# Thirty-two modulation blocks of a two-layer diffusion backbone: TensorE products in the attention stages in place of VectorE sums in the first layer's FFN

## The chip, the cores and the metric

One core of one Trainium2 chip runs the kernel. The metric is device time in microseconds (us) of one execution. Engines are TensorE (PE, its weight loads PEld), VectorE (DVE), ScalarE (ACT), GpSimd (POOL) and SyncE (SP), which here only issues DMAs. DMAs that POOL and ACT issue have queues of their own.

## What is computed

Two layers over 128 context tokens and 512 latent tokens (640 columns, width 1024). Each layer has a modulation vector for each of the two token groups, and all its norms, gates and residual adds use it:

```
mod = silu(cond) @ w_ada + b_ada                # 6 x 1024 values per layer and group
sh1, sc1, g1, sh2, sc2, g2 = split(mod, 6)
h = rmsnorm(x) * (1 + sc1) + sh1
x = x + g1 * (sum_b sigmoid(gate_b) * branch_b(h)) @ w_out     # retention, differential attention, MLA
h = rmsnorm(x) * (1 + sc2) + sh2
x = x + g2 * (silu(h @ w_a) * (h @ w_b)) @ w_ffn_out           # SwiGLU, 22 tiles of 128
```

In the kernel the 6144 values of a layer are 48 blocks of 128 columns of `w_ada`: blocks 0 to 15 are sh1 and sc1, 16 to 23 g1, 24 to 39 sh2 and sc2, 40 to 47 g2.

## The kernel before

Everything is held transposed, features on the 128 partitions, and the 640 tokens in two halves of 320. A large matmul is three products of fp32r parts (hi·hi, hi·lo, lo·hi; `mm3`, L134). A weight piece (512 KB for 1024 columns) is loaded by `load_w` through SP into a ring of three buffers, `raw`; ACT casts it to `whi` (L118) and DVE subtracts to `wlo` (L121), which frees the ring buffer. `whi` and `wlo` are rings of four.

Stages of a layer: MLA attention (with the projections of differential attention, `diff_proj`, as fillers), first branch, differential attention (fillers: gates and retention values), retention, the last branch, `out_proj`, and the FFN. Fillers are generators; `plan` spreads their steps over the points of a stage at which `fill` is called. What a filler yields goes to PSUM bank `G`, of which there is one. A scheduler then decides each engine's order; engines run their own instructions strictly in that order.

Modulation blocks are made in two ways.

- `ada_chunk` (L214 to L226), at the start of the program: four blocks at a time. Eight fp32 products (L218) with the two condition vectors as 32 weight columns (`cs`), two for each of four column groups of TensorE, give 512 columns in `G`. ACT copies that to `ada_r` (L221), four products with a selecting matrix (L224) bring it to columns, DVE adds the bias. First layer, blocks 0 to 15.
- `ada_rows` (L238 to L259): one block at a time on DVE. POOL loads the block transposed (`rawr`, 512 KB); two multiplications by a broadcast condition vector with a running sum (L251, `junk` is the unused product) give the block for both groups.

`ada_rows` is called in each layer's last branch and `out_proj` for blocks 16 to 39 (and 40 to 43 of the first layer), with 1024 columns at a time. Blocks 44 to 47 of the first layer and 0 to 15 and 40 to 47 of the second are made in the first layer's FFN, in halves of 512 columns (two loads of 256 KB, four DVE instructions a block). The second layer's FFN has none.

The FFN (`ffn`, L1228) makes the 22 tiles in parts: after a part's up products (`up`), its down products (`unit`) run between the next part's. Each part adds to the residual `x` on DVE (`x_add`, L1082), from `G` or `O`; a new accumulation there waits for that add. From tile `FFN_CLASSIC` on, `ffn_seven` uses seven products of half size in place of eight. The two layers differ: `FFN_PARTS`, `FFN_HELD` and `FFN_CLASSIC` are tables by layer (seven parts and classic until tile 5 in the first layer, six parts and until tile 4 in the second), so that the loads and sums have room in SBUF.

Of the kernel before, what the change touches and what calls it, by code (L numbers as in the profile page):

```python
# [12 lines left out]
F32 = mybir.dt.float32  # L13
# [8 lines left out]
P = 128  # L22
D = 1024
KT = 8
DEPTH = 2
# [13 lines left out]
FFN_PARTS = (((0, 3), (3, 6), (6, 9), (9, 12), (12, 15), (15, 18), (18, 22)), ((0, 4), (4, 8), (8, 12), (12, 15), (15, 18), (18, 22)))  # L39
FFN_HELD = (6, 7)  # L40
FFN_CLASSIC = (5, 4)
# [10 lines left out]
class Kern:  # L52
# [185 lines left out]
    def ada_rows(self, l, b0, b1, pool, raws, cols, bufs):  # L238

        d = self.dve  # L240
        if l not in self.mod:
            self.mod[l] = self.const.tile([P, 48, 2], F32, name=f"mod{l}")
        mod = self.mod[l]
        part = self.const.tile([P, 48, 2], F32, tag="modp", name="modp", bufs=1) if cols < 1024 else None
        for n in range(b0, b1):
            for c in range(0, 1024, cols):
                raw = raws.tile([P, cols], F32, tag="rawr", name="rawr", bufs=bufs)
                self.pool.dma_start(out=raw, in_=self.io["w_adat"][l, n][:, c:c + cols])
                junk = pool.tile([P, cols], mybir.dt.bfloat16, tag="junk", name="junk")
                for i in range(2):  # L250
                    self.tc.keep_in_program_order(d.scalar_tensor_tensor(  # L251
                        junk, raw, 1.0, self.csr[:, i, c:c + cols], op0=ALU.mult, op1=ALU.mult,
                        accum_out=(part if c else mod)[:, n, i:i + 1]))
            if n == b1 - 1:
                b = self.pv[:, V_ADA + 48 * l + b0:V_ADA + 48 * l + b1]
                if part is not None:
                    d.tensor_tensor(mod[:, b0:b1], mod[:, b0:b1], part[:, b0:b1], op=ALU.add)
                d.tensor_tensor(mod[:, b0:b1], mod[:, b0:b1], b.unsqueeze(2).to_broadcast([P, b1 - b0, 2]), op=ALU.add)
            yield 1  # L259
# [963 lines left out]
    def ffn(self, l, act, x, pool, hook, a, b, mid, us=None):  # L1223
# [21 lines left out]
        def hold(f):  # L1245
            g[f] = (pool.tile([P, T], F32R, tag="ghi", name="ghi", bufs=FFN_HELD[l]), pool.tile([P, T], F32R, tag="glo", name="glo", bufs=FFN_HELD[l]))

# [18 lines left out]
        def up(f):  # L1266
            if us is not None and f >= FFN_CLASSIC[l]:
                W = self.ffn_weights(pool, io["w_ffn_in"][l, f])
                self.fill()
                if f == FFN_CLASSIC[l]:  # L1270
                    self.pin = True
                    self.sctx.close()
                    if l == 1:
                        self.adctx.close()
# [15 lines left out]
        for p, (f0, f1) in enumerate(FFN_PARTS[l]):  # L1290
            nf, lastp = f1 - f0, p == len(FFN_PARTS[l]) - 1

# [18 lines left out]
            for f in range(max(f0, 2), f1):  # L1311
                up(f)
                for _ in range(min(2 if lastp and nf < FFN_HELD[l] - 2 else 3, len(waiting))):
                    waiting.pop(0)()
# [30 lines left out]
    def run(self):  # L1345
# [3 lines left out]
        for l in range(DEPTH):  # L1349
# [12 lines left out]
            with ExitStack() as c2:  # L1362
                pool = self.sb("mla", 1, c2)
                self.plan(37, (self.diff_proj(l, act, pool), 30, 0.0, 1.0))
                self.mla(l, act, yraw, pool, first)
                self.flush()
# [8 lines left out]
            self.plan(23, (self.gates(l, 2, act, m, mp), 16, 0.0, 0.7), (self.ret_values(l, act, mp), 20, 0.6, 0.95))  # L1375
# [22 lines left out]
            def mdone(h):  # L1398
                mact[h] = self.m_split(m, h)
            self.ada_vectors(adp, rp)  # L1400
            self.plan(22, (chain(self.ada_rows(l, 16, 24, adp, rp, 1024, 3), self.ada_rows(l, 24, 40, adp, rp, 1024, 3)), 24, 0.0, 0.9),
                      *([(self.ada_rows(0, 40, 44, adp, rp, 1024, 3), 4, 0.9, 1.0)] if l == 0 else []))
# [6 lines left out]
            us = [fp.tile([P, T], F32, tag=("ghi", "glo")[k % 2], name="us", bufs=FFN_HELD[l]) if k < 6 else  # L1409
# [11 lines left out]
            if l == 0:  # L1421
                self.plan(72, (self.ada_rows(0, 44, 48, adp, fp, 512, 2), 4, 0.0, 0.0277),
                          (chain(self.ada_rows(1, 0, 16, adp, fp, 512, 2), self.ada_rows(1, 40, 48, adp, fp, 512, 2)), 24, 0.12, 0.9))
# [73 lines left out]
def layout(inputs):  # L1497
# [22 lines left out]
    out["w_ada"] = c(np.stack([pieces(wa[:, 512 * j:512 * j + 512], 2) for j in range(4)]).reshape(1, 4, 4, 128, 2, 512))  # L1520
    out["w_adat"] = c(g["w_ada"].transpose(0, 2, 1).reshape(DEPTH, 48, 128, 1024))
# [53 lines left out]
```

## Time and profile before

| | |
|---|---|
| median of 3 runs | 2491.19 us (2485.24 to 2496.12) |
| the profiled execution | 2487.97 us, of which the span from first to last instruction is 2485.8 us |
| busy share: PE, PEld, DVE, ACT, POOL | 96%, 93%, 74%, 44%, 7% |
| mean granted TensorE clock | 0.992 |
| DMA | 250 MB, mean 101 GB/s |

The profile's PE time is that of pipelined matmuls with modelled ends, so 96% does not say that PE never waits; the start of one matmul to the start of the next is what is read below. The first layer runs from 0 to some 1266 us of the span, the second from there to the end.

### The profile page before, as it was taken

To read this page: it belongs to the slowest core of one execution; us is meant where nothing else is said; L and a number is where in the kernel's file an instruction comes from. 1 tells how busy PE (TensorE), PEld (TensorE's weight loads), DVE (VectorE), ACT (ScalarE), POOL (GpSimd) and SP (SyncE) were. 2 spreads that over 40 slices of the span, in tenths; PEclk is the share of its full clock that TensorE was granted. 3 is DMA by queue.
4 is the path that set the end of the run, shared out by engine and by line. 5 is a ranking of instruction groups with operands and counts; after the bars stand their busy time and mean duration, and the time that the engine had idled before them with its cause. 6 is when DMAs were issued, how large, how long until landed. Compare 5 with 4: busy or idle time off the path is not lost.

```text
span 2485.8 us, 43255 instructions
## 1 busy us (share of the span) xinstructions
PE 2383.3 (96%) x16816; PEld 2315.5 (93%) x16816; DVE 1840.8 (74%) x4146; ACT 1092.2 (44%) x2259; POOL 170.9 (7%) x295
## 2 busy tenths in 40 slices
PE   8999999999999999899999999999999999999997
PEld 5999998999998999899999999989999999999997
DVE  5877686566798788888778776865667976777775
ACT  5655565532234333333365664654222353333344
POOL 0000210000110000000000002100001100000001
PEclk9999999999999999999999999999999999999998
DMA  6211321321653333233232122223225512222222
GB/s 263 74 61 62 102 82 56 109 88 60 208 187 114 96 113 115 96 111 116 82 129 71 65 71 97 81 68 107 74 85 195 186 53 86 76 81 79 77 75 72
DMA packets 83180, 250.03 MB, mean 101 GB/s; under 512 B 11200, under 2 KB 24736, under 8 KB 81952
## 3 DMA queue, kind: packets, MB, share of 16 engines
q1 hardware_dynamic: 55008, 164.13, 20.6%
q0 software_dynamic: 21920, 77.17, 9.4%
q10 hardware_dynamic: 6048, 5.98, 0.7%
q8 instruction: 132, 2.16, 0.4%
q14 instruction: 72, 0.59, 0.1%
HBM read 227.01 MB, written 20.22 MB: 99 GB/s over the span
## 4 chain that ended last, share of the span: by engine, by line
PE 73%; issue 11%; DVE 9%; DMA 4%; ACT 3%; POOL 0%; DVEq 0%; POOLq 0%; ACTq 0%
PE G L134 32%; PE S L134 22%; PE Tp L134 4%; DMA rawr<-w_adat 2%; PE O L872 2%; PE S L1122 1%; PE Tp L675 1%; PE S L1121 1%; PE S L1120 1%; DVE wlo L121 1%; DVE junk L251 1%; DVE x L1082 1%; PE O L650 1%; DMA raw<-w_ffn_in 1%; PE O L649 1%
## 5 line engine op out<-in xcount | busy, mean ns | idle before, releaser
L118 ACT CAST whi<-raw 128x1024 fp32r<-128x1024 f32 (+3 forms) x354 | 298.1, 844 | 475.2 <-PE S L134 185.0
L121 DVE TENSOR_TENSOR wlo<-raw,whi 128x1024 fp32r<-128x1024 f32 (+3 forms) x354 | 342.2, 968 | 101.0 <-ACT whi L118 97.3
L134 PE MATMUL G<-whi,hhi 128*128 128x256 f32 x1040 | 299.0, 288 | 4.7 <-DVE rvs L825 2.9
L134 PE MATMUL G<-whi,hlo 128*128 128x256 f32 x1040 | 295.2, 284 | 0.0
L134 PE MATMUL G<-wlo,hhi 128*128 128x256 f32 x1040 | 294.5, 283 | 0.0
L134 PE MATMUL G<-ghi,whi 128*128 128x320 f32 x704 | 223.3, 317 | 26.5 <-DVE x L1082 23.5
L134 PE MATMUL G<-glo,whi 128*128 128x320 f32 x704 | 219.5, 312 | 0.3 <-DVE glo L121 0.3
L134 PE MATMUL G<-ghi,wlo 128*128 128x320 f32 x704 | 219.2, 311 | 0.0
L251 DVE SCALAR_TENSOR_TENSOR junk<-rawr,csr 128x512 bf16<-128x512 f32 (+1 forms) x216 | 204.1, 945 | 16.0 <-DMA rawr<-w_adat 14.3
L134 PE MATMUL S<-hhi,whi 128*128 128x320 f32 x652 | 204.4, 314 | 5.8 <-DVE gt L1049 5.7
L134 PEld LDWEIGHTS G<-whi,hhi 128*128 128x128 f32 x1040 | 198.1, 191 | 8.1 <-DVE rvs L825 3.8
L134 PE MATMUL S<-hhi,wlo 128*128 128x320 f32 x652 | 202.3, 310 | 0.0
L134 PE MATMUL S<-hlo,whi 128*128 128x320 f32 x652 | 202.3, 310 | 0.0
L134 PEld LDWEIGHTS G<-wlo,hhi 128*128 128x128 f32 x1040 | 198.5, 191 | 0.1
L134 PEld LDWEIGHTS G<-whi,hlo 128*128 128x128 f32 x1040 | 198.3, 191 | 0.0
L1082 DVE SCALAR_TENSOR_TENSOR x<-G,mod,x 128x128 f32<-128x128 f32 (+2 forms) x360 | 147.3, 436 | 38.2 <-PE G L134 37.2
L134 PEld LDWEIGHTS G<-ghi,whi 128*128 128x128 f32 x704 | 133.8, 190 | 37.3 <-issue 26.6
L134 PE MATMUL G<-hhi,whi 128*128 128x320 f32 x512 | 161.9, 317 | 5.9 <-DVE x L1082 2.6
L134 PE MATMUL G<-hlo,whi 128*128 128x320 f32 x512 | 158.9, 310 | 0.0
L134 PE MATMUL G<-hhi,wlo 128*128 128x320 f32 x512 | 158.7, 310 | 0.0
L465 DVE TENSOR_REDUCE mx<-S 128x1 f32<-128x640 f32 (+1 forms) x160 | 113.4, 715 | 50.5 <-PE S L843 29.3
L134 PEld LDWEIGHTS G<-glo,whi 128*128 128x128 f32 x704 | 134.0, 190 | 0.7 <-DVE glo L121 0.6
(439 smaller groups left out, 6632.9 us busy)
## 6 DMA issues: line engine op xcount, KB each, us to landing
raw<-w_ffn_in SPq DMA_DIRECT2D x88, 512.0 KB, 3.6
rawr<-w_adat POOLq DMA_DIRECT2D x52, 512.0 KB, 4.2
raw<-w_gate SPq DMA_DIRECT2D x48, 512.0 KB, 3.7
rawr<-w_adat POOLq DMA_DIRECT2D x56, 256.0 KB, 3.3
raw<-w_diff SPq DMA_DIRECT2D x24, 512.0 KB, 3.8
raw<-w_branch SPq DMA_DIRECT2D x24, 512.0 KB, 3.5
raw<-w_ret SPq DMA_DIRECT2D x24, 512.0 KB, 4.0
raw<-w_ffn_out SPq DMA_DIRECT2D x64, 192.0 KB, 2.4
```

The lines of the kernel that those rows point to most:

```text
L118: (eng or self.act).copy(hi, src)
L121: (eng or self.dve).tensor_tensor(lo, src, hi.bitcast(F32), op=ALU.subtract)
L134: ins = self.pe.matmul(*args, **kw)
L251: self.tc.keep_in_program_order(d.scalar_tensor_tensor(junk, raw, 1.0, self.csr[:, i, c:c + cols], op0=ALU.mult, op1=ALU.mult, accum_out=( ...
L465: self.dve.tensor_reduce(mx, sv, axis=AX.XY if len(sv.shape) == 3 else AX.X, op=ALU.max)
L649: self.pe.matmul(o[:, :n], vv, hi, start=i == 0, stop=False)
L650: self.pe.matmul(o[:, :n], vv, lo, start=False, stop=i == m - 1)
L675: self.pe.transpose(t[:, 256 * kb + 128 * i:256 * kb + 128 * i + 128], ps[i][:, 128 * (k0 + kb):128 * (k0 + kb) + 128], self.ident)
L872: pe.matmul(o[:, :128], at[:, 128 * kb:128 * kb + 128], V[:, kb0 + kb, :], start=kb == 0, stop=kb == nk - 1)
L1082: self.dve.scalar_tensor_tensor(x[h][:, n, c0:c1], ps[:, c0:c1], g[:, n, gi:gi + 1], x[h][:, n, c0:c1], op0=ALU.mult, op1=ALU.add)
L1120: self.pe.matmul(o, lh, rh, start=k == 0, stop=False)
L1121: self.pe.matmul(o, lh, rl, start=False, stop=False)
```

## The change

It takes 32 blocks off `ada_rows` and makes them with a new generator, `ada_products`, in groups of four blocks. A group is `ada_chunk`'s arithmetic, but it loads its four pieces (512 KB each, `rawp`) through the same three-buffer ring `raw` that the other weights use, and is a filler in two steps: eight products and the copy, then the selection and the bias. Six groups run in the first layer (four in MLA, two in differential attention), two in the second layer's MLA. The FFN tables become one set, the second layer's, for both. `ada_rows` keeps blocks 16 to 39 of each layer, spread over 21 points of the last branch and `out_proj` in place of 22 times 0.9.

```diff
-FFN_PARTS = (((0, 3), (3, 6), (6, 9), (9, 12), (12, 15), (15, 18), (18, 22)), ((0, 4), (4, 8), (8, 12), (12, 15), (15, 18), (18, 22)))
-FFN_HELD = (6, 7)
-FFN_CLASSIC = (5, 4)
+FFN_PARTS = ((0, 4), (4, 8), (8, 12), (12, 15), (15, 18), (18, 22))
+FFN_HELD = 7
+FFN_CLASSIC = 4
...
+    def ada_products(self, pool, chunks):
+
+        for l, j in chunks:
+            ps = self.G()
+            for i in range(4):
+                raw = self.w.tile([P, 2, 512], F32, tag="raw", name="rawp", bufs=3)
+                self.nc.sync.dma_start(out=raw, in_=self.io["w_adap"][l, j, i])
+                for kk in range(2):
+                    k = 2 * i + kk
+                    g = k % 4
+                    self.pe.matmul(ps[32 * g:32 * g + 32, :], self.cs[:, k, :], raw[:, kk, :],
+                                   start=k < 4, stop=k >= 4, tile_position=(0, 32 * g))
+            r = pool.tile([P, 512], F32, tag="ada_r", name="ada_r", bufs=1)
+            self.act.copy(r, ps)
+            yield 1
+            ps = self.Tp()
+            for c in range(4):
+                self.pe.matmul(ps[:, 2 * c:2 * c + 2], r[:, 128 * c:128 * c + 128],
+                               self.ct[:, C_SEL:C_SEL + 2], start=True, stop=True)
...
-                self.plan(37, (self.diff_proj(l, act, pool), 30, 0.0, 1.0))
+                chunks = ((0, 10), (0, 11), (1, 0), (1, 1)) if l == 0 else ((1, 10), (1, 11))
+                self.plan(37, (self.diff_proj(l, act, pool), 30, 0.0, 1.0), (self.ada_products(pool, chunks), 2 * len(chunks), 0.0, 1.0))
...
+            chunks = ((1, 2), (1, 3)) if l == 0 else ()
...
+                      (self.ada_products(mp, chunks), 2 * len(chunks), 0.0, 0.7))
...
-            self.plan(22, (chain(self.ada_rows(l, 16, 24, adp, rp, 1024, 3), self.ada_rows(l, 24, 40, adp, rp, 1024, 3)), 24, 0.0, 0.9),
-                      *([(self.ada_rows(0, 40, 44, adp, rp, 1024, 3), 4, 0.9, 1.0)] if l == 0 else []))
+            self.plan(21, (chain(self.ada_rows(l, 16, 24, adp, rp), self.ada_rows(l, 24, 40, adp, rp)), 24))
...
-                self.plan(72, (self.ada_rows(0, 44, 48, adp, fp, 512, 2), 4, 0.0, 0.0277),
-                          (chain(self.ada_rows(1, 0, 16, adp, fp, 512, 2), self.ada_rows(1, 40, 48, adp, fp, 512, 2)), 24, 0.12, 0.9))
+                self.plan(0)
```

How the instructions stand on three engines follows. First SP's queue in the first layer's MLA, from the first projection weights on; the names are ring buffers, and a wait on PE or DVE is for the engine that frees the buffer. Before:

```order
L126 DMA raw_840<-w_diff 128x1024 [waits DMAHW5_49,DMAHW2_49,DVE_49]
L126 DMA raw_987<-w_qp 128x768 [waits DMAHW6_49,DMAHW3_49,DVE_49]
L126 DMA raw_1124<-w_qk 128x640 [waits DMAHW7_49,DMAHW4_49,DVE_49]
L126 DMA raw_1195<-w_v 128x512 [waits DMAHW5_49,DMAHW0_49,DVE_49]
L126 DMA raw_1336<-w_diff 128x1024 [waits DMAHW6_49,DVE_49]
```

With the change:

```order
L126 DMA raw_840<-w_diff 128x1024 [waits DMAHW5_49,DMAHW2_49,DVE_49]
L265 DMA rawp_903<-w_adap 128x1024 [waits DMAHW6_49,DMAHW3_49,DVE_49]
L265 DMA rawp_907<-w_adap 128x1024 [waits DMAHW7_49,DMAHW4_49,DVE_49]
L265 DMA rawp_911<-w_adap 128x1024 [waits DMAHW5_49,DMAHW0_49,DVE_49]
L265 DMA rawp_915<-w_adap 128x1024 [waits DMAHW6_49,PE_49]
L126 DMA raw_1006<-w_qp 128x768 [waits DMAHW7_49,PE_49]
L126 DMA raw_1143<-w_qk 128x640 [waits DMAHW0_49,PE_49]
L126 DMA raw_1214<-w_v 128x512 [waits DMAHW1_49,PE_49]
```

A group's first three pieces fill the ring; its fourth, and the three weight loads behind it, wait until PE has used them. The same holds for all eight groups.

Second, PE at the same place of the program with the change: the first group, between transposes of MLA's query (`cqn`), and the first users of `w_qp` (`whi_1008`) and `w_qk` (`whi_1145`).

```order
L269 MATMUL G_902<-rawp_907,cs_86 32x512 [waits DMAHW7_49]
L269 MATMUL G_902<-rawp_907,cs_86 32x512
L269 MATMUL G_902<-rawp_911,cs_86 32x512 [waits DMAHW0_49]
L269 MATMUL G_902<-rawp_911,cs_86 32x512
L576 MATMUL Tp_956<-ct_76,cqn_953 128x128 [waits DVE_49]
L576 MATMUL Tp_956<-ct_76,cqn_953 128x128 x2
L576 MATMUL Tp_969<-ct_76,cqn_966 128x128 [waits DVE_49]
L576 MATMUL Tp_969<-ct_76,cqn_966 128x128 x2
L269 MATMUL G_902<-rawp_915,cs_86 32x512 [waits DMAHW1_49]
L269 MATMUL G_902<-rawp_915,cs_86 32x512
```

Six products stand together, then six transposes, then the two of the fourth piece. In the second layer's first group nothing stands between (`whi_14937` is `w_qk`):

```order
L269 MATMUL G_14916<-rawp_14925,cs_86 32x512 [waits DMAHW2_49]
L269 MATMUL G_14916<-rawp_14925,cs_86 32x512
L269 MATMUL G_14916<-rawp_14929,cs_86 32x512 [waits DMAHW3_49]
L269 MATMUL G_14916<-rawp_14929,cs_86 32x512
L134 MATMUL S_14941<-ckh_14350,whi_14937 128x384 [waits Activation_49]
```

Third, DVE in the first layer's FFN, at one tile of `ffn_seven` (`wlo`, `tlo`, `ts` are weights, `v` the tile, `x` the residual). Before:

```order
L251 SCALAR_TENSOR_TENSOR junk,mod_10302<-rawr,csr 128x512
L1082 SCALAR_TENSOR_TENSOR x_7883<-G,mod_191,x_7883 128x128
L1082 SCALAR_TENSOR_TENSOR x_7883<-G,mod_191,x_7883 128x192
L121 TENSOR_TENSOR tlo<-raw,thi 128x1024
L1082 SCALAR_TENSOR_TENSOR x_7885<-G,mod_191,x_7885 128x320
L251 SCALAR_TENSOR_TENSOR junk,mod_10302<-rawr,csr 128x512
L121 TENSOR_TENSOR wlo<-raw,whi 128x384
L251 SCALAR_TENSOR_TENSOR junk,modp<-rawr,csr 128x512
```

With the change (the adds' line is now L1104):

```order
L1104 SCALAR_TENSOR_TENSOR x_8034<-G,mod_191,x_8034 128x128
L1104 SCALAR_TENSOR_TENSOR x_8034<-G,mod_191,x_8034 128x192
L1104 SCALAR_TENSOR_TENSOR x_8036<-G,mod_191,x_8036 128x320
L121 TENSOR_TENSOR tlo<-raw,thi 128x1024
L121 TENSOR_TENSOR wlo<-raw,whi 128x512
```

The sums are gone from both FFNs, and PE's order in the first layer's FFN is now the second layer's. One unit of `ada_rows` (block 39) moves to the end of `out_proj`, ahead of the second norm, in both layers.

## Rows read from the trace of the kernel before

**Rows 1.** The page, busy time of the engines (us, share of the span, instructions).

```profile
PE 2383.3 (96%) x16816; PEld 2315.5 (93%) x16816; DVE 1840.8 (74%) x4146; ACT 1092.2 (44%) x2259; POOL 170.9 (7%) x295
```

**Rows 2.** Chain of waits, first `out_proj` matmuls of the two layers (start, us, what).

```profile
741.70 35.48 PE G L134 x240
...
1977.99 36.78 PE G L134 x249
```

**Rows 3.** Timeline of PE, last down product of each FFN (start, us, engine, line).

```profile
1266.32 0.31 PE L134 MATMUL G<-ghi,wlo 128*128 128x320 f32 x1
...
2468.05 0.31 PE L134 MATMUL G<-ghi,wlo 128*128 128x320 f32 x1
```

**Rows 4.** Waits of PE, `out_proj` and FFN, first layer, then second (us, times, longest).

```profile
PE G L134 <- DVE x L1082: 23.0, 23, 3.8
...
PE G L134 <- DVE x L1082: 3.2, 9, 0.7
```

**Rows 5.** Lines of DVE by form, first layer's `out_proj` and FFN.

```profile
L251 DVE SCALAR_TENSOR_TENSOR junk<-rawr,csr 128x512 bf16<-128x512 f32 x112 | 77.1, 688 | 15.4 <-DMA rawr<-w_adat 14.3 <-DVE junk L251 0.4
```

**Rows 6.** Busy us by stretch: PE, PEld, DVE, ACT, POOL, PEclk, DMA share, GB/s.

```profile
56.00:290.00 234.00, 228.14 (x1765) 221.78 (x1765) 171.56 (x426) 141.11 (x344) 27.64 (x49) 1.00 0.22 70
290.00:487.00 197.00, 188.32 (x1427) 183.38 (x1426) 132.56 (x355) 113.28 (x299) 18.62 (x30) 1.00 0.25 75
1290.00:1518.00 228.00, 221.94 (x1716) 215.30 (x1715) 168.07 (x416) 138.46 (x339) 25.06 (x45) 1.00 0.22 71
741.70:1266.50 524.80, 493.38 (x3259) 484.42 (x3260) 438.74 (x889) 189.52 (x312) 32.76 (x61) 0.99 0.34 108
1978.00:2468.20 490.20, 483.73 (x3246) 477.87 (x3246) 357.61 (x609) 193.07 (x309) 1.37 (x3) 1.00 0.24 76
```

**Rows 7.** Timeline of PE, `ada_chunk`: products (eight as x16, two as x4), selection (four as x8).

```profile
23.40 1.05 PE L218 MATMUL G<-raw,cs 128*32 128x512 f32 x4
24.38 0.81 PE L366 MATMUL Tp<-nsq,ct 128*128 128x320 f32 x2
...
42.94 0.95 PE L224 MATMUL Tp<-ct,ada_r 128*128 128x2 f32 x8
43.74 0.44 PE L381 MATMUL S<-wlo,hhi 128*128 128x416 f32 x1
...
46.69 0.35 PE L381 MATMUL O<-wlo,hhi 128*128 128x416 f32 x1
46.88 0.35 PE L382 MATMUL O<-whi,hlo 128*128 128x416 f32 x1
47.16 1.92 PE L218 MATMUL G<-raw,cs 128*32 128x512 f32 x16
49.02 0.45 PE L380 MATMUL S<-whi,hhi 128*128 128x416 f32 x1
49.31 0.35 PE L381 MATMUL S<-wlo,hhi 128*128 128x416 f32 x1
```

**Rows 8.** DMA issues, first layer's MLA, 56 to 290 us (count, KB each, us to landing).

```profile
raw<-w_diff SPq DMA_DIRECT2D x10, 512.0 KB, 3.8
...
raw<-w_qk SPq DMA_DIRECT2D x4, 320.0 KB, 2.9
```

**Rows 9.** Timeline of PE, two matmuls of 256 columns in the first layer's MLA.

```profile
125.32 0.28 PE L650 MATMUL O<-ptl,vhl 128*128 128x256 f32 x1
125.44 0.28 PE L649 MATMUL O<-pth,vhl 128*128 128x256 f32 x1
```

**Rows 10.** Lines of ACT by form, 0 to 740 us.

```profile
L118 ACT CAST whi<-raw 128x1024 fp32r<-128x1024 f32 x66 | 69.3, 1050 | 101.5 <-PE S L134 71.7 <-PE G L134 24.8 <-issue 2.9
```

**Rows 11.** Timeline of PE, first layer's FFN, from a wait on.

```profile
1198.69 0.43 PE L134 MATMUL G<-ghi,whi 128*128 128x320 f32 x1 [1.93 <-DVE x L1082]
1198.92 0.47 PE L134 MATMUL G<-glo,whi 128*128 128x320 f32 x1
...
1202.35 0.31 PE L134 MATMUL G<-ghi,wlo 128*128 128x320 f32 x1
```

More of the change, by code (lines that the diff above doesn't have):

```diff
@@ L236, in ada_vectors, with mod_tile, ada_rows @@
             d.tensor_scalar(cs[:, i, :], th, 0.5, None, op0=ALU.mult)
-    def ada_rows(self, l, b0, b1, pool, raws, cols, bufs):
-        d = self.dve
+    def mod_tile(self, l):
         if l not in self.mod:
             self.mod[l] = self.const.tile([P, 48, 2], F32, name=f"mod{l}")
-        mod = self.mod[l]
-        part = self.const.tile([P, 48, 2], F32, tag="modp", name="modp", bufs=1) if cols < 1024 else None
+        return self.mod[l]
+    def ada_rows(self, l, b0, b1, pool, raws):
+        d = self.dve
+        mod = self.mod_tile(l)
@@ L245, in ada_rows @@
         for n in range(b0, b1):
[L246 to L253, printed above, removed]
+            raw = raws.tile([P, 1024], F32, tag="rawr", name="rawr", bufs=3)
@@ L254, in ada_rows @@
+            self.pool.dma_start(out=raw, in_=self.io["w_adat"][l, n])
+            junk = pool.tile([P, 1024], mybir.dt.bfloat16, tag="junk", name="junk")
+            for i in range(2):
+                self.tc.keep_in_program_order(d.scalar_tensor_tensor(
+                    junk, raw, 1.0, self.csr[:, i, :], op0=ALU.mult, op1=ALU.mult, accum_out=mod[:, n, i:i + 1]))
             if n == b1 - 1:
                 b = self.pv[:, V_ADA + 48 * l + b0:V_ADA + 48 * l + b1]
-                if part is not None:
-                    d.tensor_tensor(mod[:, b0:b1], mod[:, b0:b1], part[:, b0:b1], op=ALU.add)
@@ L258, in ada_rows @@
                 d.tensor_tensor(mod[:, b0:b1], mod[:, b0:b1], b.unsqueeze(2).to_broadcast([P, b1 - b0, 2]), op=ALU.add)
+            yield 1
[12 more added lines that the diff above has]
+            self.act.copy(r, ps)
+            yield 1
+            ps = self.Tp()
+            for c in range(4):
+                self.pe.matmul(ps[:, 2 * c:2 * c + 2], r[:, 128 * c:128 * c + 128],
+                               self.ct[:, C_SEL:C_SEL + 2], start=True, stop=True)
+            b = self.pv[:, V_ADA + 48 * l + 4 * j:V_ADA + 48 * l + 4 * j + 4]
+            self.dve.tensor_tensor(self.mod_tile(l)[:, 4 * j:4 * j + 4, :], ps[:, 0:8].rearrange("p (a v) -> p a v", v=2),
+                                   b.unsqueeze(2).to_broadcast([P, 4, 2]), op=ALU.add)
@@ L1245, in hold @@
         def hold(f):
-            g[f] = (pool.tile([P, T], F32R, tag="ghi", name="ghi", bufs=FFN_HELD[l]), pool.tile([P, T], F32R, tag="glo", name="glo", bufs=FFN_HELD[l]))
+            g[f] = (pool.tile([P, T], F32R, tag="ghi", name="ghi", bufs=FFN_HELD), pool.tile([P, T], F32R, tag="glo", name="glo", bufs=FFN_HELD))
         def load(f):
@@ L1266, in up @@
         def up(f):
-            if us is not None and f >= FFN_CLASSIC[l]:
+            if us is not None and f >= FFN_CLASSIC:
                 W = self.ffn_weights(pool, io["w_ffn_in"][l, f])
                 self.fill()
-                if f == FFN_CLASSIC[l]:
+                if f == FFN_CLASSIC:
                     self.pin = True
                     self.sctx.close()
-                    if l == 1:
-                        self.adctx.close()
+                    self.adctx.close()
                     state["xf"] = ExitStack()
@@ L1289, in ffn @@
         waiting = []
-        for p, (f0, f1) in enumerate(FFN_PARTS[l]):
-            nf, lastp = f1 - f0, p == len(FFN_PARTS[l]) - 1
+        for p, (f0, f1) in enumerate(FFN_PARTS):
+            nf, lastp = f1 - f0, p == len(FFN_PARTS) - 1
             def dload(n, p=p, f0=f0, nf=nf):
@@ L1312, in ffn @@
                 up(f)
-                for _ in range(min(2 if lastp and nf < FFN_HELD[l] - 2 else 3, len(waiting))):
+                for _ in range(min(2 if lastp and nf < FFN_HELD - 2 else 3, len(waiting))):
                     waiting.pop(0)()
@@ L1374, in run @@
             self.branch_first(l, 2, yhi, ylo, m)
-            self.plan(23, (self.gates(l, 2, act, m, mp), 16, 0.0, 0.7), (self.ret_values(l, act, mp), 20, 0.6, 0.95))
+            chunks = ((1, 2), (1, 3)) if l == 0 else ()
+            self.plan(23, (self.gates(l, 2, act, m, mp), 16, 0.0, 0.7), (self.ret_values(l, act, mp), 20, 0.6, 0.95),
+                      (self.ada_products(mp, chunks), 2 * len(chunks), 0.0, 0.7))
             with ExitStack() as c2:
@@ L1408, in run @@
             fp = self.sb("ffn", 1, fctx)
-            us = [fp.tile([P, T], F32, tag=("ghi", "glo")[k % 2], name="us", bufs=FFN_HELD[l]) if k < 6 else
+            us = [fp.tile([P, T], F32, tag=("ghi", "glo")[k % 2], name="us", bufs=FFN_HELD) if k < 6 else
                   fp.tile([P, T], F32, tag=("thi", "tlo")[k % 2], name="us", bufs=2) for k in range(KT)]
@@ L1520, in layout @@
     out["w_ada"] = c(np.stack([pieces(wa[:, 512 * j:512 * j + 512], 2) for j in range(4)]).reshape(1, 4, 4, 128, 2, 512))
+    out["w_adap"] = c(np.stack([[pieces(g["w_ada"][l][:, 512 * j:512 * j + 512], 2) for j in range(12)] for l in L]).reshape(DEPTH, 12, 4, 128, 2, 512))
     out["w_adat"] = c(g["w_ada"].transpose(0, 2, 1).reshape(DEPTH, 48, 128, 1024))
```

## Prediction

> **What bounds the kernel now.** I read the page's busy times first: PE is busy 96% of the span [rows 1], so the question is where PE is not at its pace, and what it would have to do more. Next the chain of waits and PE's timeline, for the same stretch in both layers: from the first `out_proj` matmul to the last down product of the FFN [rows 2, 3]. It takes 1266.32 − 741.70 = 524.6 us in the first layer and 2468.05 − 1977.99 = 490.1 us in the second. The waits of PE say what the difference is: in the first layer 23 waits for the residual add `x`, 23.0 us, in the second nine, 3.2 us [rows 4]. The adds are late because DVE, which does its work in order, has the sums in front of them: 112 of 0.688 us in halves [rows 5]; DVE is busy 438.7 of 524.8 us there, against 357.6 of 490.2 [rows 6]. The waits cost more than their length. After the one that ends at 1198.69, 14 matmuls take 3.66 us [rows 11], where 240 take 35.48, 0.148 each [rows 2]: 1.6 us are lost at the lower level of the granted clock, 1.2 GHz, before the pace is back at 1202.35. Last, busy times by stretch where the products are to stand: in the first layer's MLA, its differential attention and the second layer's MLA PE is idle 5.9, 8.7 and 6.1 us, 20.7 in all [rows 6], by its modelled ends. PE is the bound there too.
>
> **The change, part by part.**
>
> *The FFN.* Both layers now have the same tables, no sums and the same order on PE, so I give the first layer the second's time: −34.6 us. The unit of `ada_rows` that moves to the end of `out_proj` puts one block more in front of the second norm's DVE work; DVE has idle time there, and I take 0.3 us a layer: +0.6. Should it come late, the norm waits for at most its multiplications, four halves of 0.688 us or 2.8 us [rows 5]. Together −34.0; the smaller end is the waits alone, 23.0 − 3.2 = 19.8 [rows 4], if the rest of the difference came from the tables.
>
> *PE's new work.* A group's eight products stand as six and two. Eight took 49.02 − 47.16 = 1.86 us, and two alone 24.38 − 23.40 = 0.98 [rows 7]: two column groups take as long as four. So six take 1.86, and a group 2.84; eight groups 22.7. The selection took 43.74 − 42.94 = 0.80; eight are 6.4. Products are on a 128×32 tile and all around them on 128×128. From `O` to the products the step was 0.28, back to the next matmul 0.29, where the pace is 0.19 [rows 7]: 0.1 a change. Seven groups change four times and one twice, 30 × 0.1 = 3.0. Sum +32.1, all on the path, since PE is the bound and none of this can lie beside its other work. The copy on ACT and the bias on DVE stand behind it; the fillers leave many steps between, so they cost nothing while ACT keeps its idle half.
>
> The Trainium skill (TensorEngine Tiling (Array Packing), Tiling Modes) says that changing the tiling mode drains TensorE. Taking a drain as the matmul's 0.35 less its pace of 0.19 [rows 7], 0.16 a change, the 30 would cost 4.8 instead of 3.0; the row's step, with both effects in it, decides.
>
> *The fourth piece.* The ring has three buffers. The fourth piece is issued once the first two products are over, some 1.0 us after the group's start, and lands 3.8 us later, as 512 KB do in this stage [rows 8]: at 5.0 with its issue. Six products end at 1.9, so PE would wait 3.1 us, less the work that stands between: 6, 25, 20, 18, 12, 5, 0 and 14 matmuls in the eight groups by the order, at some 0.114 each (0.12 for 256 columns [rows 9], many have 128). That is 8 × 3.1 − 100 × 0.114 = +13.4. The ends are 0 (PE is slowed there anyway by softmax on DVE and ACT) and 8 × 3.1 = 24.8.
>
> The Trainium skill (DMA: Bandwidth & Descriptors, Anatomy of one DMA) has a fit of 2.0 us plus bytes at 436 KB per us for a transfer that GpSimd issues; 512 KB would then land in 3.2 instead of 3.8, an estimate by which this term were 4.8 less. Rows 8 are of SP's own queue, and decide.
>
> *The weights behind it.* The loads of `w_qp`, `w_qk`, `w_v` and `w_gate` queue on SP behind the fourth piece and land 2.9 to 3.8 us after their own release [rows 8], then ACT casts for up to 1.05 us [rows 10]. In four groups (first, fifth, sixth and the second layer's first) a user follows within 5 us; I take 2.0, 1.1, 1.2 and 1.4 us of wait, and 0.2 in the rest: +5.9. The sixth group's selection is one of them: it waits for a copy that stands behind a cast. Ends 0 and 16 (2 us a group).
>
> *The clock.* Three of the stalls come out at 2.4 to 3.1 us, longer than the 1.93 of rows 11. Each may bring the 1.6 us of rows 11: +4.8, ends 0 and 4.8.
>
> *What comes back.* PE's idle 20.7 us are mostly waits for DVE and ACT in softmax. Products or stalls that come just before such a wait fill it; those before nothing don't. I take half, −10.3, ends 0 and −20.7.
>
> Sum: 32.1 + 13.4 + 5.9 + 4.8 − 10.3 = 45.9 against 34.0: **+11.9 us**. On the profiled execution's 2487.97 that is 2499.9, say **2500**. This execution is 3.2 us under the median of the runs shown, 2491.19, within their spread; 0.5%, some 12.5 us, is about what a measurement of this kernel can tell from no change, so "the same" is 2479 to 2504.
>
> **The rivals.**
>
> *No stalls: faster.* The microseconds in which the fourth piece is awaited are ones in which PE waits for softmax anyhow, so the three stall terms vanish, and the products fill between half and all of the idle time. For it: rows 6 show 20.7 us of idle time by modelled ends, and true ends may be earlier. Against it: in the second layer's first group nothing stands between the sixth and the seventh product, and the first has six transposes. Time: 2488.0 + 32.1 − 34.0 less 10.3 to 20.7 = 2465 to 2476, middle 2471.
>
> *The ring of three decides: slower.* The idle time is elsewhere than the groups, nothing comes back, and the four pieces hold up SP in every group: +32.1 + 13.4 + 5.9 + 4.8 − 34.0 = +22.2, 2510; with the upper end of the weights' term it is 2520. It wins over the forecast from the point where less than 6 us of the idle time is filled. For it: PE is busy 97.5% of the first MLA stretch [rows 6], and queued loads are in order. Against it: seven groups have work in between, and a softmax chain that is late has slack behind it.
>
> *The change does not shorten the FFN.* The first layer's FFN could be long for something other than the sums. Then all of the cost stays: 2488.0 + 45.9 = 2534. Waits on `x` of 23.0 against 3.2 us [rows 4], with the lower clock behind them, speak against it; little speaks for it.
>
> **How the numbers follow.** The forecast has 0.43, within 0.5%; on its own it would range from 2486 to 2504. The first rival has 0.20, the second 0.33, the third 0.04. So faster by over 0.5%: 0.20; within: 0.43; slower: 0.37. The range reaches from the middle of the first rival to the upper value of the second, 2470 to 2520, and leaves out the third and the far ends.
>
> **What would show it.** In the changed kernel's profile: the stretch from the first `out_proj` matmul to the last down product near 490 us in the first layer, and few waits for `x`; the products as 1.86 and 0.98; a wait for a DMA before the seventh product of a group, up to 3.1 us, longest in the second layer's first group; the first layer's stretch from 56 us to the end of differential attention longer by some 32 us, and the second layer's MLA by 10 or more. Wrong I would be if the seventh product found its piece in place, if the first FFN stayed over 500 us, or if MLA grew by less than the products' own 4 us a group.

## The result, and the profile after

The changed kernel takes 2520.24 us (median of 4 runs, 2513.84 to 2522.42) against 2489.49 before: ratio 1.0117, 95% interval 1.0087 to 1.0147. It is slower by 1.2%. The forecast was 2500, no change that a measurement can tell; the result lies at the upper end of the stated range, where the second rival had put it. The profiled execution took 2521.40 us, its span 2519.6: 33.8 us longer than the span before, where the sum said 11.9.

First the changed kernel's page, busy times as in [rows 1], and its chain by engine:

```profile
PE 2415.9 (96%) x16996; PEld 2330.6 (93%) x16996; DVE 1769.7 (70%) x3883; ACT 1102.4 (44%) x2265; POOL 139.1 (6%) x235
...
PE 81%; DVE 9%; ACT 3%; issue 3%; DMA 3%; POOL 0%; DVEq 0%; ACTq 0%; SPq 0%; POOLq 0%
```

DVE has lost 71 us of work, PE has gained 32.6. The chain of waits of the changed kernel, the first `out_proj` matmuls, as in [rows 2]:

```profile
777.71 36.78 PE G L134 x249
...
2013.22 36.79 PE G L134 x249
```

Busy times by stretch, as in [rows 6]: first layer's MLA, its differential attention, the second layer's MLA, then `out_proj` and FFN of the first and of the second layer:

```profile
56.00:319.40 263.40, 254.55 (x1923) 238.96 (x1923) 178.20 (x436) 145.60 (x354) 29.94 (x52) 0.99 0.30 99
319.40:537.70 218.30, 205.60 (x1574) 195.88 (x1573) 142.12 (x399) 117.43 (x307) 18.26 (x28) 1.00 0.32 103
1291.50:1565.60 274.10, 255.98 (x1883) 243.00 (x1882) 177.66 (x432) 147.46 (x354) 30.09 (x52) 0.97 0.26 83
777.70:1266.50 488.80, 482.19 (x3246) 476.32 (x3246) 361.28 (x616) 190.79 (x304) 2.13 (x4) 1.00 0.27 83
2013.20:2502.00 488.80, 482.22 (x3246) 476.32 (x3246) 359.87 (x613) 193.39 (x309) 1.90 (x4) 1.00 0.25 77
```

The first three stretches end where the stages do; those of [rows 6] end 9 to 19 us sooner, so lengths are to be compared in the table below and not here. The two FFNs are alike: 488.7 and 488.6 us from matmul to matmul. In the first, PE's waits for the residual add have gone from 23.0 us to the 4.4 of this row of its waits [rows 4]:

```profile
PE G L134 <- DVE x L1104: 4.4, 11, 0.7
```

To see where the rest went, PE's timeline of both kernels is divided at the same matmuls, from the first one of a stage to the first one of the next (the FFN ends with its last down product; "boundary" is from there to the second layer's first projection). Microseconds longer than before:

| stretch | first layer | second layer |
|---|---|---|
| MLA | +20.2 (four groups) | +28.1 (two groups) |
| differential attention | +11.1 (two groups) | −0.1 |
| retention | 0.0 | 0.0 |
| last branch | +4.7 | +3.6 |
| `out_proj` and FFN | −36.0 | −1.4 |
| boundary between the layers | +3.6 | |

With signs this sums to +33.8. The first layer's totals are what was forecast, 31.3 us more in the attention stages ("some 32") and 36 less in the FFN, the first of them by errors that cancel (below). The surprise is the second layer: its MLA has two groups and grew by more than the first layer's with four.

**A group as forecast.** PE's timeline in the changed kernel, the first layer's first group and the second layer's first (a profile x12 is six products, x4 two):

```profile
84.52 1.91 PE L269 MATMUL G<-rawp,cs 128*32 128x512 f32 x12
86.36 0.55 PE L576 MATMUL Tp<-ct,cqn 128*128 128x128 f32 x3
...
89.46 1.05 PE L269 MATMUL G<-rawp,cs 128*32 128x512 f32 x4 [1.10 <-DMA rawp<-w_adap]
...
1340.50 1.91 PE L269 MATMUL G<-rawp,cs 128*32 128x512 f32 x12 [0.51 <-ACT stg L830]
1345.50 1.05 PE L269 MATMUL G<-rawp,cs 128*32 128x512 f32 x4 [3.09 <-DMA rawp<-w_adap]
1347.86 0.69 PE L134 MATMUL S<-ckh,whi 128*128 128x384 f32 x1 [1.31 <-ACT whi L118]
```

Six products take 86.36 − 84.52 = 1.84 us, and the second layer's first group waits 3.09 us for its fourth piece and 1.31 for the cast of `w_qk` (forecast: 1.86, 3.1, 1.4). The chain of waits shows the same group from link to link (start, us, what):

```profile
1340.50 1.09 PE G L269 x8
1341.59 3.86 DMA rawp<-w_adap
1345.45 0.04 issue
1345.50 1.08 PE G L269 x4
1346.60 0.58 ACT ada_r L272
1347.18 0.63 ACT whi L118
1347.82 0.04 issue
1347.86 1.65 PE S L134 x4
```

Two products free the buffer after 1.09 us, and the piece lands 3.86 later. Over all eight groups PE waited before the products for (us, times):

```profile
  DMA rawp<-w_adap: 9.6, 7
```

**What was not forecast** comes behind that group. Busy times by stretch of 4 us (PE, PEld, DVE, ACT, POOL, then the granted clock):

```profile
1344.00:1348.00 4.00, 1.19 (x5) 0.29 (x5) 0.16 (x1) 1.40 (x3) 0.00 (x0) 0.81 0.66 226
1348.00:1352.00 4.00, 4.00 (x14) 4.00 (x15) 1.27 (x2) 0.33 (x1) 0.00 (x0) 0.50 0.83 294
...
1360.00:1364.00 4.00, 2.03 (x15) 1.83 (x15) 3.74 (x11) 2.20 (x8) 0.00 (x0) 0.94 0.33 110
1364.00:1368.00 4.00, 4.00 (x22) 3.96 (x21) 2.97 (x9) 1.67 (x4) 0.00 (x0) 0.63 0.05 22
```

After the stall PE runs at 1.2 GHz (0.50), has little work from 1360 to 1364, and then its granted clock falls to that level again. The matmul at 1362.82 has waited 1.97 us for the exponentials of the first softmax, in PE's timeline:

```profile
1360.58 0.28 PE L134 MATMUL G<-whi,ckl 128*128 128x256 f32 x1
1362.82 0.55 PE L134 MATMUL S<-kt,qt 96*128 96x128 f32 x3 [1.97 <-ACT pp L489]
```

What should stand beside that softmax is the projections of differential attention, the fillers. The order has used them up: in the second layer's MLA 72 of their hi·hi products stand ahead of the first `S<-ckh,whi`, where before it were 48; between that matmul and the first scores there are none, where before it were 8, and none from there to the first transpose of probabilities, where before it were 16. The keys and values of MLA's second projection (`ckh`) start at 1347.86, 34.1 us later than before, 30.5 counted from the stage's first matmul, and that delay is made good only in part.

### The profile page after: what moved, and what is told of

Read it like the earlier page. It is cut to its first block, busy times and chain, and to the rows that moved or that the text cites. A ratio compares the mean times of both kernels' runs of the same rounds, so it can differ in the third digit from the quotient of the medians.

```text
span 2519.6 us, 43242 instructions
## 1 busy us (share of the span) xinstructions
PE 2415.9 (96%) x16996; PEld 2330.6 (93%) x16996; DVE 1769.7 (70%) x3883; ACT 1102.4 (44%) x2265; POOL 139.1 (6%) x235
## 4 chain that ended last, share of the span: by engine, by line
PE 81%; DVE 9%; ACT 3%; issue 3%; DMA 3%; POOL 0%; DVEq 0%; ACTq 0%; SPq 0%; POOLq 0%
PE G L134 33%; PE S L134 26%; PE Tp L134 7%; PE O L894 1%; PE S L1144 1%; PE S L1143 1%; PE S L1142 1%; PE Tp L697 1%; DVE wlo L121 1%; DVE x L1104 1%; ACT whi L118 1%; DMA rawp<-w_adap 1%; DVE v L1241 1%; PE G L269 1%; PE O L672 1%
## 5 line engine op out<-in xcount | busy, mean ns | idle before, releaser
L118 ACT CAST whi<-raw 128x1024 fp32r<-128x1024 f32 (+4 forms) x346 | 295.9, 858 | 463.8 <-PE S L134 174.2
L121 DVE TENSOR_TENSOR wlo<-raw,whi 128x1024 fp32r<-128x1024 f32 (+4 forms) x346 | 340.1, 985 | 138.6 <-ACT whi L118 136.8
L1104 DVE SCALAR_TENSOR_TENSOR x<-G,mod,x 128x128 f32<-128x128 f32 (+2 forms) x336 | 137.1, 436 | 41.9 <-PE G L134 40.7
L487 DVE TENSOR_REDUCE mx<-S 128x1 f32<-128x640 f32 (+1 forms) x160 | 113.0, 714 | 43.3 <-PE S L865 24.8
L134 PEld LDWEIGHTS S<-hhi,whi 128*128 128x128 f32 x656 | 125.4, 191 | 13.7 <-DVE gt L1071 13.5
## 6 DMA issues: line engine op xcount, KB each, us to landing
raw<-w_ffn_out SPq DMA_DIRECT2D x64, 256.0 KB, 2.7
```

The costliest lines, as they stand in the source:

```text
L118: (eng or self.act).copy(hi, src)
L121: (eng or self.dve).tensor_tensor(lo, src, hi.bitcast(F32), op=ALU.subtract)
L134: ins = self.pe.matmul(*args, **kw)
L487: self.dve.tensor_reduce(mx, sv, axis=AX.XY if len(sv.shape) == 3 else AX.X, op=ALU.max)
L1104: self.dve.scalar_tensor_tensor(x[h][:, n, c0:c1], ps[:, c0:c1], g[:, n, gi:gi + 1], x[h][:, n, c0:c1], op0=ALU.mult, op1=ALU.add)
```

## The experiments

All runs are timed against the kernel before; the times of stretches are those of one profiled execution, divided as in the table above. For the same work they differ between runs: the first layer's differential attention with its two groups and a ring of three is 10.4 to 13.7 us longer than before in the four kernels that have it, and the last branches, where no group stands, are 0 to 4.8 us longer with a ring of three.

**Without the groups.** In all three places `chunks = ()`, and the blocks set to zero.

> The changed kernel with the eight groups left out: their 32 blocks are set to zero, so the modulation is incomplete. It measures the gain alone, and by its distance to the changed kernel's 2520 us the whole price of the groups. If the groups' price is what the prediction summed (45.9 us), it takes 2520 - 46 = 2474; if the price is what the stretches of the changed kernel's trace add up to (20 + 11 us in the first layer, 28 in the second layer's MLA, 59 in all), 2461. The late landing of csr in the two last branches (a wait of 3.3 and 4.0 us before a matmul of S in place of 1.7 and 2.2) should be gone if the groups cause it, and stay if the new spread of the sums does.

Measured: 2459.19 us, ratio 0.9878 (0.9853 to 0.9902). MLA and differential attention are within 0.4 us of before in both layers. So the gain alone is some 29 us, and the groups cost 2520.2 − 2459.2 = 61, not 46. The boundary stays 4.2 us longer and both last branches 2.7: that much belongs to other parts of the change, not to the groups.

**A ring of four.**

```diff
-        raw = self.w.tile([P, cols], F32, tag="raw", name="raw", bufs=3)
+        raw = self.w.tile([P, cols], F32, tag="raw", name="raw", bufs=4)
```

(and the same number for `rawp` and for `ts`).

> The changed kernel with the ring raw of four buffers in place of three, for all weights and for the pieces. All eight products of each group then stand together in PE's order. Theory one, the ring: the fourth piece is in flight with the others, so the waits for it (9.6 us in the changed kernel's trace, 7 times), the waits for weights behind it and the stretches at 1.2 GHz after them go away: 15 to 25 us, 2495 to 2505. Theory two, the place: what a group costs beyond its own PE work is the order around it (projections used up ahead of it, then a softmax that nothing covers); the ring is worth 5 us or less, 2515.

Measured: 2501.18, ratio 1.0043 (1.0029 to 1.0056), 19 us less than the changed kernel. No wait of a product for a DMA is left. But by stretch it is not one theory or the other. The first layer's MLA stays at +21.0: there the ring was worth nothing. Its differential attention falls from +11.1 to +5.9, the second layer's MLA from +28.1 to +19.8, and the last branches from +4.7 and +3.6 to −0.5 and +1.5, which no group touches (below). Two groups still cost the second layer 19.8 us without a single wait for a piece; PE waits 2.7 us there for the cast of `w_qk`, whose load still stands behind the pieces.

**The second layer's groups in differential attention**, with the ring of three: `chunks = ()` in its MLA, `((1, 10), (1, 11))` in its differential attention.

> The changed kernel with the second layer's two groups moved from its MLA to its differential attention, where the first layer has two as well; the ring stays at three. If the 28 us that the second layer's MLA grew by belong to the place (the first group stands where nothing covers the wait, with the weights of the next scores behind it), the two groups cost the 11 us that they cost in the first layer's differential attention: 2520 - 17 = 2503. If they belong to the groups wherever they stand, it stays within 5 us of 2520.

Measured: 2508.72, ratio 1.0072 (1.0049 to 1.0094). That MLA falls from +28.1 to +3.4, differential attention rises to +13.3. The place matters, by 11.4 us over both stretches; two groups cost 13.3 in the second layer's differential attention with this ring, and 10.4 to 13.7 in the first's (13.7 in this run).

**Three waiting down units a tile.**

```diff
-                for _ in range(min(2 if lastp and nf < FFN_HELD - 2 else 3, len(waiting))):
+                for _ in range(min(2 if lastp and l == 1 else 3, len(waiting))):
```

> The changed kernel with one number put back: in the last part of the first layer's FFN three waiting down units a tile are taken, as before the change, and not two. ACT's order then has no table loads between the norm's operations at the end of that FFN (the changed kernel has four of 1.28 us there, the kernel before none). If the 3.7 us that this boundary grew by come from these loads, 2520 - 3.7 = 2516; if from something else, no difference at the boundary.

Measured: 2518.90, ratio 1.0108 (1.0078 to 1.0138). The boundary is where it was before (−0.2). ACT's timeline in the changed kernel, the norm's operations at the end of the first FFN with the first two of the four loads:

```profile
1263.42 1.28 ACT L315 ACT_TABLE_LOAD   x1
1264.71 0.53 ACT L315 ACTIVATE nr<-Tp,epsc 128x320 f32<-128x320 f32 x1
1265.14 0.47 ACT L304 ACTIVATE nsq<-x 128x320 f32<-128x320 f32 x1
1265.62 1.28 ACT L316 ACT_TABLE_LOAD   x1
1266.92 0.47 ACT L316 ACTIVATE nr<-nr 128x320 f32<-128x320 f32 x1
```

and in this kernel, where no load stands between them:

```profile
1265.59 0.52 ACT L315 ACTIVATE nr<-Tp,epsc 128x320 f32<-128x320 f32 x1
1266.01 0.46 ACT L304 ACTIVATE nsq<-x 128x320 f32<-128x320 f32 x1
1266.37 0.46 ACT L316 ACTIVATE nr<-nr 128x320 f32<-128x320 f32 x1
```

In the changed kernel the first matmul behind the boundary waits for what ACT makes next, the normed input `hhi`, in PE's timeline:

```profile
1268.61 0.46 PE L1142 MATMUL S<-whi,hhi 128*128 128x416 f32 x1 [1.93 <-ACT hhi L333]
```

Here that wait is gone; so the loads were the cause at the boundary. But the FFN ahead of it is 2.4 us longer, so little is left: giving both layers the same tables gave the first also the second's table loads, and the tables that avoid them cost nearly as much.

**All groups in differential attention**, ring of four: six in the first layer's, two in the second's; their span there ends at 0.9 and not at 0.7.

> The ring of four, and all eight groups in differential attention: six in the first layer's, two in the second's, none in MLA. With the ring of four the two groups in the first layer's differential attention cost 5.9 us over before, 3.0 each, and those in MLA 5.3 and 9.9 each. Theory one, the place: a group in differential attention costs its PE work of about 3 us anywhere there: 2459 + 8 x 3 = 2483, with both MLA stretches as before the change. Theory two, crowding: six groups in one stretch meet each other and the gates there, and a group costs 5 us or more again: 2500, no better than with the ring alone.

Measured: 2489.41, ratio 1.0000 (0.9990 to 1.0011). Between the two theories, and both are seen. In the second layer that stretch is 1.4 us longer and MLA 1.8. The 1.8 is no idle time of PE: 120 matmuls of the first branch (`yhi`, `ylo`) stand ahead of the transpose that ends the stretch, where before it were 108, and twelve at 0.148 are 1.8 us. Together 3.2 us, less than the two groups' PE work of 5.3: idle time is filled. In the first layer six cost 34.6, where their work is 6 × (1.86 + 0.80) = 16. PE's idle time there grows by 11.0 us, and the granted clock is at 0.5 for 17 us, where before it never was. At the head of its waits stands one in differential attention's own chain (us, times, longest), which was 1.1 us in two times before:

```profile
PE Tp L908 <- DVE osb L903: 5.9, 1, 5.9
```

**The same with fewer groups**: blocks 40 to 43 of both layers as sums in the last branch again.

```diff
-            self.plan(21, (chain(self.ada_rows(l, 16, 24, adp, rp), self.ada_rows(l, 24, 40, adp, rp)), 24))
+            self.plan(21, (chain(self.ada_rows(l, 16, 24, adp, rp), self.ada_rows(l, 24, 44, adp, rp)), 28))
```

> As the last, but in each layer the first four blocks of g2 (40 to 43) are made by sums on DVE in the last branch and out_proj again, as before the change in the first layer, so that six groups are left, five in the first layer's differential attention and one in the second's. If DVE has room for four more blocks there (9.8 us of sums a layer against some 17 us of idle time in the hundred before out_proj), 2459 + 6 x 3 = 2477; if not, the last branch or the norm behind out_proj grows by up to 10 us a layer, 2490 or more.

Measured: 2489.38, ratio 0.9998 (0.9988 to 1.0007). The four blocks cost nothing that I can see (last branches −0.2 and −2.3, `out_proj` and FFN within 0.6 us of the run before it). But five groups in the first layer's differential attention cost 34.8, as much as six. So it is not the count alone. That the place of the groups against the chains of that stage decides is likely and not shown: which group does it there I did not try.

**The second layer's groups later**, ring of four: `0.0 if l == 0 else 0.4` as the start of their span in MLA.

> The ring of four, places as in the changed kernel, but the second layer's two groups begin at 0.4 of its MLA and not at 0. With the ring of four that MLA was 19.8 us longer than before. If that is the price of the first group standing ahead of the first scores, where projections are used up in front of it and the first softmax then has nothing beside it, it falls to the two groups' PE work and a little, 6 to 9 us: 2501 - 12 = 2489. If a group costs 10 us anywhere in MLA, it stays near 20 and 2501.

Measured: 2484.75, ratio 0.9980 (0.9969 to 0.9991). That MLA is 8.0 us longer than before in place of 19.8. Nothing else was moved, so the early place was worth 11.8 us. Both groups start later, counted from the stage's first matmul: the first by 69 us, the second by some 12. That it is the first group's place that counts is read from the trace.

**The same move with the ring of three**, to see whether the two add up.

> The changed kernel with its ring of three; only the second layer's two groups begin at 0.4 of its MLA. Its first group then has 21 rows of other work between the sixth and the seventh product, where the changed kernel has none. With the ring of four the same move was worth 11.8 us in that stretch. If place and ring add up, the stretch is 28.1 - 11.8 = 16 us longer than before and the kernel takes 2508; if the cover between the products makes the ring harmless there, it is some 8 us longer, as with the ring of four, and the kernel takes 2500.

Measured: 2502.70, ratio 1.0049 (1.0031 to 1.0067). The stretch is 9.1 us longer than before, not 16: in this stretch they don't add up. PE's timeline there, the second layer's first group:

```profile
1412.54 1.91 PE L269 MATMUL G<-rawp,cs 128*32 128x512 f32 x12
1414.38 0.39 PE L671 MATMUL O<-pth,vhl 128*128 128x256 f32 x1
...
1418.68 1.05 PE L269 MATMUL G<-rawp,cs 128*32 128x512 f32 x4
1419.66 0.44 PE L697 MATMUL Tp<-ct,p 128*128 128x128 f32 x2
```

Between the sixth product and the seventh lie 4.3 us of other work, and no wait is left; the one other wait for a piece in this stretch is 0.9 us. With the first group out of the way, `S<-ckh,whi` starts at 1320.43 and not at 1347.86, with 48 fillers ahead of it as before the change.

**Put together.** Ring of four, blocks 40 to 43 as sums, six groups: three late in the first layer's MLA (from 0.3 of it on), two in its differential attention, one in the second's; three units a tile.

```diff
-                chunks = ((0, 10), (0, 11), (1, 0), (1, 1)) if l == 0 else ((1, 10), (1, 11))
+                chunks = ((0, 11), (1, 0), (1, 1)) if l == 0 else ()
...
-            chunks = ((1, 2), (1, 3)) if l == 0 else ()
+            chunks = ((1, 2), (1, 3)) if l == 0 else ((1, 11),)
```

> Put together: the ring of four; in each layer blocks 40 to 43 as sums in the last branch; the remaining six groups three in the first layer's MLA from 0.3 of it on, two in its differential attention, one in the second layer's differential attention; and three waiting down units a tile in the first FFN's last part. From the stretches: 2459 without groups, three late groups in MLA at 4 each (two late ones cost the second layer 8.0), two in differential attention 4.4, one in the second layer's 2: 2477, faster than before by 12. If the price of a group in MLA is not that of its early place, 3 x 5.3 in place of 12 and 2481.

Measured: 2475.79, ratio 0.9945 (0.9929 to 0.9961): faster than before by 0.55% and than the changed kernel by 44 us. Its stretches: the first layer's MLA +15.1, differential attention +7.5, `out_proj` and FFN −32.9, boundary +0.5; the second layer's MLA +5.3, without a group in it. Of the last, 1.8 us are again the twelve matmuls ahead of the split; the granted clock is at 0.5 twice for 3.4 us there (from 1325.7 and 1510.0), where before it never was, an estimate of 3.2 us more at the 1.6 us that 3.4 us of it cost in [rows 11]. What brought the clock down I don't know: PE's idle time in the stretch is as before.

**One step further**: blocks 40 to 47 as sums, four groups.

> As the last, but blocks 40 to 47 of each layer as sums in the last branch and out_proj, so that four groups are left: two in the first layer's MLA from 0.4 of it on and two in its differential attention; none in the second layer. If DVE still has room, 2459 + 8 + 4.4 = 2471. If it has not (19.6 us of sums more a layer than the changed kernel, against some 17 us of idle time in the hundred before out_proj), the norm behind out_proj waits, 5 to 10 us a layer: 2481 to 2491.

Measured: 2478.94, ratio 0.9955 (0.9939 to 0.9971), no better than the last, whose interval it overlaps. Fewer groups save 7.3 us in the first layer's attention stages and 1.7 in the second's, but `out_proj` and FFN are 6.4 and 4.7 us longer: by that, DVE has no room left for eight more blocks ahead of the second norm.

## Why the prediction was right and wrong

**Right: the gain.** −34.0 was forecast for the FFN, `out_proj` and what lies behind; the three stretches sum to −36.0 + 3.6 − 1.4 = −33.8. The third rival is gone. PE's idle time there falls by 24.8 us, 18.6 of them waits for `x`; the granted clock was at 0.5 for four times 3.4 us there before and never after, an estimate of 6.4 us more at the 1.6 of [rows 11]. No run tells the sums from the tables that changed with them, so the rest of the 36.0 is open. The size is partly luck: the FFN gained 1.4 us more than the second layer's old time, and the boundary took back 3.6 for ACT's table loads, which I had not counted when I gave one layer the other's tables.

**Right: a group by itself.** Products 1.84 and 0.99 against 1.86 and 0.98 (1474.10 to 1475.09 in the timeline), the selection 0.81 against 0.80. The Trainium skill's rule of the drain (TensorEngine Tiling (Array Packing), Tiling Modes) is not told apart from the step of 0.1 us by these numbers: six products lie with their change within 0.02 us of the row. The fourth piece lands 3.86 us after its issue, as [rows 8] said with 3.8. The Trainium skill's fit for GpSimd's transfers (DMA: Bandwidth & Descriptors, Anatomy of one DMA) is for another queue; by it the piece would land in an estimated 3.2 us and the wait of 3.09 be 2.4, and the measured 3.86 decides.

**Right in mechanism, too large: the waits for the fourth piece and for weights.** 13.4 us was forecast for the pieces, 9.6 measured, 7 of 8 groups. The longest is exactly the one with nothing in between. The pieces come when worked out, the seventh product starting 4.8 to 5.3 us after the group (5.0 was forecast). The work between took longer than 0.114 us a matmul: six transposes take 2.0 us in the first group, with a wait of their own. For the weights behind them 5.9 us was forecast; PE's waits for the cast of a weight in the stretches with groups are 1.4 us in the first layer's differential attention and 1.3 in the second layer's MLA.

**Too small: the clock.** I counted three stalls with 1.6 us each. In the stretches with groups there are five places where the granted clock falls to 0.5, from 90.4 and 1346.5 for 6.8 us each and from 1363.6, 1476.2 and 1547.9 for 3.4: 24 us in all, before the change none. At the 1.6 us that 3.4 us of it cost in [rows 11], that is an estimate of 11 us, against 4.8. Two of the five are no stall of a group: the one at 1363.6 follows the uncovered softmax, and the one at 1547.9 stands 70 us behind the last products, after 8 us in which PE was busy for 4.9.

**Wrong: the second layer's MLA.** My terms for its two groups sum to 15.6 us (2 × 3.64 and 0.6 of PE's work and changes, 4.6 of stalls, 1.5 of weights, 1.6 of clock); it took 28.1. What I had costed is there. What I had not is the step itself, the first group's early place: the order puts three blocks of fillers in front of the group, the projections for the first scores start 30.5 us late, and the first softmax has nothing beside it. The order of PE that stands ahead of the prediction, where `S<-ckh,whi` follows on the eight products, showed half of it; I read there what PE would wait for, and not what had been taken from the place behind. With the same ring and the same loads the stretch is 9.1 us longer once the groups stand later; with the ring of four and no wait for a piece left it is still 19.8 at the early place. What the step costs can be read from PE's idle time and clock. This stretch before the change, and with the groups later (ring of three), as in [rows 6]:

```profile
1287.90:1533.90 246.00, 239.65 (x1836) 232.73 (x1835) 175.54 (x430) 145.64 (x352) 30.05 (x52) 1.00 0.23 76
...
1294.50:1549.60 255.10, 248.74 (x1884) 236.99 (x1882) 176.26 (x432) 147.19 (x354) 30.45 (x52) 0.99 0.28 90
```

PE idles 6.4 us in both, and 274.1 − 256.0 = 18.1 in the changed kernel, 11.8 more. Of these, 6.0 are the stalls that I had costed, 4.7 for the pieces and 1.3 for the cast; the rest is waits that I had not. The longest in PE's waits there (us, times, longest):

```profile
PE G L269 <- DMA rawp<-w_adap: 4.7, 2, 3.1
PE S L134 <- ACT pp L489: 2.0, 1, 2.0
PE Tp L697 <- DVE ptl L121: 1.4, 4, 0.6
PE S L134 <- ACT whi L118: 1.3, 1, 1.3
```

The granted clock is at 0.5 for 17 us of this stretch, by the same price an estimate of 8.0 us, against my 1.6. The groups' own work is 2 × (1.84 + 0.98 + 0.81) = 7.3. Together 11.8 + 8.0 + 7.3 = 27.1 of the 28.1. With the groups later the clock is at 0.5 once, for 3.4 us, and the same sum is 0 + 1.6 + 7.3 = 8.9; 9.1 was measured.

**Wrong: "what comes back".** I let −10.3 us of idle time be filled. In the groups of the changed kernel nothing came back on balance. In the second layer's MLA PE's idle time grew: a group that starts a chain later makes idle time and doesn't fill it. In the first layer it grew too, from 14.6 us [rows 6] to 8.9 + 12.7 = 21.6, by 7.0; the waits for pieces (4.9) and for casts of weights (1.4) are 6.3 of that, so the other waits stayed as they were. That the first layer still met "some 32" is luck: its stalls were 6.3 us, not the 13 that I had costed, and this stood in for the 7 that were to come back.

**Not costed: the last branches**, +8.3 us together. Both start with the load of the broadcast condition vectors (`csr`, 1 MB, POOL's queue), and PE waits for gates behind it. This load landed later, by the DMA issues of the changed kernel (KB, us to landing):

```profile
csr<-condr POOLq DMA_DIRECT2D x2, 1024.0 KB, 7.7
```

It is the median of the two layers' loads. Before the change it was 6.1 us; without groups 7.0; with the ring of four between 5.1 and 6.2, and with the ring of three and late groups 7.9. So the groups are not its only cause: without any, 2.7 us of the last branches are still there. From the changed kernel to the ring of four the last branches account for 7 of the 19 us gained, 5 of them in the first layer. What differs there is the load's place in the order, in POOL's timeline, the first layer in the changed kernel and with the ring of four:

```profile
653.65 0.55 POOL L163 DMA_DIRECT2D csr<-condr  x1 [112.42 <-DVE gt L1071]
...
638.57 0.55 POOL L163 DMA_DIRECT2D csr<-condr  x1 [101.00 <-PE O L1003]
```

Counted from the first matmul of retention, it is issued at 115.9 in the one and at 104.5 in the other. In the nine last branches of ring-of-four kernels where it is issued at 104.5, it lands after 5.0 to 5.3 us, and PE has no wait as long as a microsecond for the gate. In all others, before the change too, it is issued at 115.9 to 116.3, lands after 5.7 to 8.4 us, and PE waits 1.4 to 4.1 us for the gate. What spreads it between 5.7 and 8.4 I don't know; the transfer shares its queue with the first block of the sums in every kernel here.

Of the rivals, the second, "the ring of three decides", gave the right time with a reason that is half right. That nothing comes back holds in the changed kernel; but by the stretches with groups the ring is worth 12.7 us (differential attention 5.2, the second layer's MLA 8.3, less 0.8 in the first's), and the place of two groups alone 19. That it was right to the microsecond is luck: it counted neither the place nor the last branches. The first rival has its case too, in one stretch: two groups in the second layer's differential attention with the ring of four cost 3.2 us, with the 1.8 that the split counts to MLA, for 2 × (1.86 + 0.80) = 5.3 us of work.

## What to carry to other kernels

When work is moved to a saturated engine as a filler, cost not only its own time but the order that it displaces: see which fillers now stand ahead of the next chain of dependent steps, and what is left to cover that chain. A transfer that has to wait for a ring buffer is harmless if work of its flight time stands between its release and its use. Here moving two groups gained 17.5 us with the ring of three, a fourth buffer alone 19.1, and both 35.5; a move costs no memory. And where two stages are made alike, the second one's boundary, table loads included, comes with it.

## What the runs showed that I had not expected

- Two groups at the start of the second layer's MLA cost 28.1 us, two at 0.4 of it 9.1, with the same loads and the same ring.
- Four groups cost the first layer's MLA 20.2 us with a ring of three and 21.0 with four, though the products waited 1.8 us for pieces in the one and never in the other.
- The same load of 1 MB took between 5.0 and 8.4 us to land in kernels with the same code for it; where it was issued 11.4 us sooner it took 5.0 to 5.3 in all nine cases, and the last branch is up to 4.8 us longer than before where it was not.
- The growth of PE's idle time, the groups' own work and the price of the time at 1.2 GHz together give what the second layer's MLA grew by to within 1 us, at both places of the groups.
- A shift of two matmul units in a program's order brought four table loads of 1.28 us to ACT at a place where PE had to wait for it.
